# A two-layer decoder trunk on one core: the order of the first loads, early throw-away products, the first shift and scale on TensorE, and the third column chunk on its own

## The chip, the cores and the metric

The kernel runs on one core of one Trainium2 chip. The metric is the device time of one execution in microseconds; the median of three runs is compared.

## The reference, cut to what matters

The input is x, 256 rows of 1,024 numbers, and a conditioning vector c. Two layers follow one another, each an attention and a gated feed-forward part. All of it is float32. Before each attention and each feed-forward part the rows are normed, scaled and shifted; scale and shift come from c:

```python
c_act = jax.nn.silu(c)
for i in range(DEPTH):                                   # DEPTH = 2
    mod = (c_act @ ada_w[i] + ada_b[i])[:, None, :]      # 1024 x 6144 weights for each layer
    sh_a, sc_a, g_a, sh_f, sc_f, g_f = jnp.split(mod, 6, axis=-1)
    h = rms_norm(x, norm_g[i, 0]) * (1.0 + sc_a) + sh_a
    y = moba_attention(h, ...) if i % 2 == 0 else diff_attention(h, ...)
    x = x + g_a * rms_norm(y, norm_g[i, 1])
    h = rms_norm(x, norm_g[i, 2]) * (1.0 + sc_f) + sh_f
    x = x + g_f * rms_norm(swiglu(h, ffn_w_in[i], ffn_w_out[i]), norm_g[i, 3])
```

Both attentions begin with h @ w_qkv, 1,024 x 3,072 weights. No row of the first product can be finished before shift and scale (sh_a, sc_a of layer 0) are known for the rows of w_qkv that it uses.

## The kernel before, in words

The 256 rows are two row tiles (t = 0, 1) of 128. A contraction of 1,024 is eight chunks of 128 (k = 0 to 7). A weight tile is loaded as float32 and split in two parts that add up to it: ACT copies the first part (line 470), VectorE subtracts (line 471). Each product is three matmuls of up to 512 columns (line 479): first part by first part, and the two mixed ones.

`first_block` (lines 664 to 688) makes q (512 columns), k (512 columns) and a third chunk, 512 more columns of q, for both row tiles. It goes over the contraction in blocks of 1, 2, 2, 2 and 1 chunks: (0, 1), (1, 2), (3, 2), (5, 2), (7, 1). For each block `ada_first` makes shift and scale of just these 128 or 256 columns: it loads the two column strips of ada_w for all 1,024 rows of c in pieces of 256 KB (line 413), multiplies the eight row chunks by their part of c and adds them up in one tile a, the first on ACT (line 383), the other seven on VectorE (line 385), and PE sums a over the partitions with a product by a column of ones (line 397). `shift_scale` adds ada_b (tile abc) and the norm's weight (tile ngc) and gives scsh (lines 374 and 377). `modulate` applies scsh to the normed, transposed x (tile xT) and splits the result into the parts of h, tile hq (ACT lines 495 and 500, VectorE line 501). Then come the products of the block, tile pq; each step of them uses the weights of q, k and the third chunk together. The third chunk is loaded for two contraction chunks at once (`qk1`).

x itself is loaded (line 314), squared and summed on ACT (line 529), its root taken on GpSimd (lines 458 to 461), scaled on VectorE (tile xh, line 509), transposed on PE (tile ph, line 326) and copied by ACT to xT (line 671). c, norm_g and ada_b come as small tiles c8, ng and ab (lines 310 to 312), are transposed on PE and copied to cact, ngc and abc (lines 333 to 335).

No order of instructions is written out by hand. `Schedule` holds all operations with an estimated cost each and gives every engine its order by list scheduling, ten passes forward and backward with a fixed seed; the order that comes out best by its estimates is issued. Each engine works its list in order; all loads go through SP's queue, small ones too. Tiles share slots by class (`raw` for loads, `ring` for split weights, `s2`, `bc` and `a` in PSUM, and so on), so that an operation can also wait for a slot. Changing one estimate can change the order everywhere in the program.

After the first block follow the rest of k, then v, the softmax, the output projection, and a feed-forward part of six column chunks; then the same for layer 1. The later shifts, scales and gates (`ada`) are summed on VectorE too, beside the products.

Of the kernel before, what the change touches and what calls it, by code (L numbers as in the profile page):

```python
# [18 lines left out]
D = 1024  # L19
# [27 lines left out]
class Buf:  # L47
    """A tile in a slot of `cls`, taken by its first operation and free after its last; kept when cls is None."""
# [9 lines left out]
class Op:  # L58
    """One or more instructions of an engine, with the estimated cost."""
    __slots__ = ("eng", "cost", "fn", "preds", "succs", "n", "prio", "thin", "start", "end", "bufs", "act", "main", "ready",  # L60
                 "idx", "name")


class Schedule:
    """Operations in program order with what they read and write. `best` gives every engine its order,
    by list scheduling over estimated costs (us)."""

    def __init__(self, slots):
        self.ops, self.slots = [], slots

    def op(self, eng, cost, fn, r=(), w=(), act=None, main=False, name=None, thin=False):
        o = Op()
        o.eng, o.cost, o.fn, o.act, o.main, o.name = eng, cost, fn, act, main, name
        o.thin, o.preds, o.succs, o.bufs, o.idx = thin, set(), [], [], len(self.ops)
        for items, wr in ((r, False), (w, True)):
# [22 lines left out]
    def latest(self):  # L98
        """latest starts before the main products"""
        main = None  # L100
        for o in reversed(self.ops):
            e = min((s.prio - self.latency(o, s) for s in o.succs), default=0.0)
            if o.main:
                e, main = min(e, main.prio if main else e), o
            o.prio = e - (o.cost + 2.5 if o.eng == "SP" else o.cost if o.eng == "PE" else o.cost * STRETCH)

    def turn(self):
        """the same schedule with time reversed"""
# [4 lines left out]
    def run(self, byprio=False):  # L113
# [19 lines left out]
        order, act = [], None  # L133

        def when(o):
            """when o can start, or None while a slot's release isn't known"""
# [15 lines left out]
        while len(order) < len(ops):  # L152
            soon, moved = [], False
            for e in ENGINES:
# [12 lines left out]
                o = min((o for _, o in can), key=lambda o: (o.prio, o.idx))  # L167
                if e in ("ACT", "DVE"):
# [7 lines left out]
                if e == "SP":  # L176
                    at[e] = now + 0.57
# [41 lines left out]
    def best(self):  # L219
        """Rounds of scheduling with time running forward and backward, each with the other's times as priorities."""  # L220
        rng, best = random.Random(SEED), None
        self.latest()
        for i in range(ROUNDS):
            for back in (False, True):
                if back:
                    self.turn()
                for _ in range(4):
                    try:
                        order = self.run(i > 0 and not back)
# [37 lines left out]
def trunk_kernel(ctx: ExitStack, tc: tile.TileContext, x, c, rel_bias, ada_w, ada_b, norm_g, moba_w_qkv, moba_w_o,  # L267
# [52 lines left out]
    def transposes(dst, dkey, blocks, r, main=False):  # L320
        """blocks: list of (column offset in dst, function giving the source)"""
# [5 lines left out]
        op("PE", 0.108 * len(blocks), f, r=list(r) + [ident], w=[(dst, dkey)], main=main, name="tr")  # L327

# [40 lines left out]
    def shift_scale(r, pg, off, l, j, k0, n):  # L369
        """columns of sums -> shift, or the norm's weight times one plus the scale"""  # L370
# [24 lines left out]
    def colsums(pg, off, a, blocks):  # L395
        for i, b in enumerate(blocks, off):
            op("PE", 0.215, lambda i=i, b=b: nc.tensor.matmul(pg[:, i:i + 1], b(), ones1.t[:], start=True, stop=True),  # L397
               r=[a, ones1], w=[(pg, K(i))], thin=True)
# [3 lines left out]
    def ada_first(k0, n):  # L402
        """shift and scale of the first norm for n contraction chunks from k0"""
        m = n * 128
        a = Buf(f"a0{k0}", "s2", [128, 2, m])
        pg = Buf(f"pg0{k0}", "bc")
        q = 4 // n
        for kc in range(0, KC, q):
# [8 lines left out]
        colsums(pg, 0, a, [lambda j=j, b=b: a[:, j, b * 128:b * 128 + 128] for j in range(2) for b in range(n)])  # L417
# [37 lines left out]
    def rstd(m0, n=1, w=1, m1=None):  # L455
        """from m0/n, or from the sum of m0 and m1, the means' halves"""
# [8 lines left out]
    def wpair(name, src, off, seg, kstride, n=512):  # L465
        """rows off.. of 128, two segments of n columns `seg` apart, in two parts that add up to them"""
# [389 lines left out]
```

## Time and profile before

| what | value |
|---|---|
| time of three runs | 650.39, 650.85, 650.94 us, median 650.85 us |
| span of the profiled execution, first to last instruction | 649.0 us, 1.85 us below that median |
| TensorE (PE) busy | 624.0 us, 96% |
| VectorE (DVE) busy | 467.5 us, 72% |
| ScalarE (ACT) busy | 374.4 us, 58% |
| moved by DMA | 160.6 MB, 247 GB/s over the span |

The span is that of one profiled execution; the times are of runs without a profile. Busy is the time in which an engine works at least one instruction. PEld is the loading of the stationary operand and runs beside PE.

### The profile page before, as it was taken

Reading aid. Unit: us, or ns where it says so; the run is one execution under the profiler, and the core shown is the slowest. Engines: PE = TensorE matmul, PEld = TensorE weight load, DVE = VectorE, ACT = ScalarE, POOL = GpSimd, SP = SyncE. Lnnn points to the kernel's source line nnn. Section 1 sums busy time; section 2 is a strip of 40 time slices with the busy share of each in tenths; the row PEclk is TensorE's granted clock in tenths of the full one; section 3 lists DMA queues with packets and bytes.
Section 4 is the critical chain, followed back from the end, with each engine's and each line's share of the span. In section 5 each row is a group of like instructions: output and inputs, shape, how many; then the busy total and the mean of one; then the engine's idle time right before and its main releaser. Section 6 shows DMA issues by size and latency. Waiting matters only on the chain.

```text
span 649.0 us, 8664 instructions
## 1 busy us (share of the span) xinstructions
PE 624.0 (96%) x3069; PEld 517.9 (80%) x3069; DVE 467.5 (72%) x587; ACT 374.4 (58%) x628; POOL 29.9 (5%) x66
## 2 busy tenths in 40 slices
PE   1799999999999999999999999999999999999996
PEld 1687878888788888888988877888888888888894
DVE  3988499997887786757588889896756454587353
ACT  3658779488373535524388878846845253444341
POOL 1000000021000000000020000211100000000001
PEclk9999999999999999999999999999999999999999
DMA  8999999999989697849558847582674738294501
GB/s 276 363 351 314 295 350 352 362 292 284 362 294 369 191 395 254 302 141 317 183 193 293 294 141 268 165 289 66 228 259 114 276 105 283 74 385 144 210 1 65
DMA packets 72488, 160.60 MB, mean 247 GB/s; under 512 B 5491, under 2 KB 22516, under 8 KB 72444
## 3 DMA queue, kind: packets, MB, share of 16 engines
q1 hardware_dynamic: 72444, 160.04, 72.1%
q8 instruction: 24, 0.39, 0.2%
q14 instruction: 20, 0.16, 0.1%
HBM read 158.69 MB, written 1.33 MB: 247 GB/s over the span
## 4 chain that ended last, share of the span: by engine, by line
PE 89%; DMA 5%; ACT 2%; DVE 1%; SPq 1%; issue 1%; DVEq 0%; POOLq 0%; POOL 0%; ACTq 0%
PE pf L479 19%; PE pg L479 17%; PE pu L479 17%; PE pq L479 13%; PE po L479 7%; PE pv L479 6%; PE po L636 2%; PE ps L590 2%; PE pa L326 1%; PE pgc L397 1%; DMA sg<-in_diff_subln_g_dram 1%; DMA x<-in_x_dram 1%; DMA bias<-toep 1%; PE ppt L326 1%; PE pqk L326 1%; DMA aw<-in_ada_w_dram 1%
## 5 line engine op out<-in xcount | busy, mean ns | idle before, releaser
L479 PE MATMUL pg<-s_i,h 128*128 128x512 f32 (+1 forms) x576 | 212.3, 375 | 0.0
L479 PE MATMUL pu<-s_i,h 128*128 128x512 f32 (+1 forms) x576 | 210.8, 373 | 0.0
L479 PE MATMUL pf<-s_u,a 128*128 128x512 f32 x528 | 128.6, 395 | 1.6 <-ACT a L770 1.6
L479 PEld LDWEIGHTS pu<-s_i,h 128*128 128x128 f32 x576 | 108.5, 188 | 19.1
L479 PEld LDWEIGHTS pg<-s_i,h 128*128 128x128 f32 x576 | 108.4, 188 | 19.2
L471 DVE TENSOR_TENSOR s_i<-w_i,s_i 128x1024 fp32r<-128x1024 f32 (+1 forms) x96 | 107.1, 1134 | 20.7 <-ACT s_i L470 17.4
L479 PEld LDWEIGHTS pf<-s_u,a 128*128 128x128 f32 x528 | 98.1, 188 | 23.5 <-ACT a L770 2.0
L470 ACT ACTIVATE s_i<-w_i 128x1024 fp32r<-128x1024 f32 (+1 forms) x96 | 93.0, 985 | 39.4 <-PE pf L479 17.7
L385 DVE SCALAR_TENSOR_TENSOR acc<-aw,cact,acc 128x1024 f32<-128x1024 f32 x70 | 89.2, 1280 | 7.0 <-DMA aw<-in_ada_w_dram 5.8
L471 DVE TENSOR_TENSOR s_u<-w_u,s_u 128x1024 fp32r<-128x1024 f32 x44 | 53.0, 1223 | 29.0 <-ACT s_u L470 28.0
L470 ACT ACTIVATE s_u<-w_u 128x1024 fp32r<-128x1024 f32 x44 | 45.7, 1057 | 36.3 <-PE pu L479 23.1
L770 ACT ACTIVATE a<-pa 128x512 fp32r<-128x512 f32 (+1 forms) x24 | 13.4, 562 | 74.6 <-PE pa L326 74.5
L479 PE MATMUL po<-s_o,o 128*128 128x512 f32 x192 | 48.2, 398 | 0.0
L479 PE MATMUL pq<-s_q,h 128*128 128x512 f32 x192 | 47.5, 398 | 0.0
L771 DVE TENSOR_TENSOR a<-pa,a 128x512 fp32r<-128x512 f32 (+1 forms) x24 | 15.3, 646 | 40.5 <-ACT a L770 40.2
L479 PEld LDWEIGHTS pq<-s_q,h 128*128 128x128 f32 x192 | 35.1, 188 | 7.9 <-issue 0.3
L471 DVE TENSOR_TENSOR s_q<-w_q,s_q 128x1024 fp32r<-128x1024 f32 x32 | 38.5, 1219 | 3.5 <-ACT s_q L470 3.5
L479 PEld LDWEIGHTS po<-s_o,o 128*128 128x128 f32 x192 | 35.2, 188 | 6.8
L470 ACT ACTIVATE s_q<-w_q 128x1024 fp32r<-128x1024 f32 x32 | 33.2, 1058 | 7.7 <-DMA w_q<-in_moba_w_qkv_dram 6.3
L479 PE MATMUL pq<-s_q,hq 128*128 128x512 f32 x144 | 37.3, 417 | 0.0
L479 PEld LDWEIGHTS pq<-s_q,hq 128*128 128x128 f32 x144 | 28.4, 201 | 6.6 <-issue 0.6
L458 POOL TENSOR_SCALAR ms<-ss 128x1 f32<-128x1 f32 x16 | 8.4, 528 | 512.2 <-ACT z L529 501.2
(124 smaller groups left out, 708.3 us busy)
## 6 DMA issues: line engine op xcount, KB each, us to landing
aw<-in_ada_w_dram SPq DMA_DIRECT2D x80, 512.0 KB
w_i<-in_ffn_w_in_dram SPq DMA_DIRECT2D x80, 512.0 KB
w_u<-in_ffn_w_out_dram SPq DMA_DIRECT2D x44, 512.0 KB
aw<-in_ada_w_dram SPq DMA_DIRECT2D x32, 256.0 KB
w_q<-in_moba_w_qkv_dram SPq DMA_DIRECT2D x16, 512.0 KB
w_q<-in_diff_w_qkv_dram SPq DMA_DIRECT2D x16, 512.0 KB
w_q0v<-in_moba_w_qkv_dram SPq DMA_DIRECT2D x8, 512.0 KB
w_o<-in_moba_w_o_dram SPq DMA_DIRECT2D x8, 512.0 KB
```

The lines of the kernel that those rows point to most:

```text
L326: nc.tensor.transpose(dst[:, o:o + n], a, ident[:n, :n])
L385: op("DVE", tt(n) + 0.065, lambda: nc.vector.scalar_tensor_tensor(a.t, w(), cact[:, kc:kc + 1], a.t, op0=OP.mult, op1=OP.add), r=[cact, w. ...
L397: op("PE", 0.215, lambda i=i, b=b: nc.tensor.matmul(pg[:, i:i + 1], b(), ones1.t[:], start=True, stop=True), r=[a, ones1], w=[(pg, K(i))], ...
L458: op("POOL", 0.16, lambda: nc.gpsimd.tensor_scalar(ms.t, m0.t[:], 1.0 / n, EPS, op0=OP.mult, op1=OP.add), r=[m0], w=[ms])
L470: op("ACT", ac(2 * n), lambda: nc.scalar.activation(b[:, 0], w.t[:], AF.Copy), r=[w], w=[(b, K(0))], name="hi" + name)
L471: op("DVE", tt(2 * n), lambda: nc.vector.tensor_sub(b[:, 1], w.t[:], b[:, 0].bitcast(F)), r=[w, (b, K(0))], w=[(b, K(1))], name="lo" + name)
L479: nc.tensor.matmul(p[:, :n], a, b[:, 1 if q == 1 else 0, s], start=first and q == 0, stop=last and q == 2)
L590: nc.tensor.matmul(p[:, i * nk:i * nk + nk], qT[rows, h0 + i, t * 128:t * 128 + 128], kT[rows, h0 + i, 0:nk], start=True, stop=True)
L636: nc.tensor.matmul(p[:, i * 128:i * 128 + 128], a, b, start=kt == 0, stop=kt == t)
L770: op("ACT", ac(n, 0, True), lambda: nc.scalar.activation(a[:, 0, :m], pv(), AF.Copy), r=[p], w=[(a, KR(0, m))])
L771: op("DVE", tt(n), lambda: nc.vector.tensor_sub(a[:, 1, :m], pv(), a[:, 0, :m].bitcast(F)), r=[p, (a, KR(0, m))], w=[(a, KR(10, m))])
```

## The change

The small tile c8 heads SP's queue, followed by the first row tile of x; ab and ng are now issued by ACT's queue. For this an operation has a `boost`, which the forward pass looks at before anything else, and a mark `dma` for loads that another engine than SP issues. Ten products of a tile of ones by itself are added, with the lowest boost, so that PE's list holds them where nothing else can be put. `ada_first` sums the first block (k0 = 0) on PE: 128 columns of ada_w as the stationary operand by one column of c, eight row chunks into one PSUM column each for shift and scale; the additions on ACT and VectorE and the tile a are gone there. The later blocks keep them. In `first_block` the products of the third column chunk are operations of their own, behind those of q and k for both row tiles. Three estimates of the scheduling change: a product, an addition and a column sum cost a little more; and the first activation table counts as loaded. Comments are dropped.

```diff
-    def op(self, eng, cost, fn, r=(), w=(), act=None, main=False, name=None, thin=False):
+    def op(self, eng, cost, fn, r=(), w=(), act=None, main=False, name=None, thin=False, boost=0, dma=False):
...
-        order, act = [], None
+        order, act = [], "silu"
...
-                o = min((o for _, o in can), key=lambda o: (o.prio, o.idx))
-                if e in ("ACT", "DVE"):
+                o = min((o for _, o in can), key=lambda o: (0 if back else -o.boost, o.prio, o.idx))
+                if e in ("ACT", "DVE") and (back or not o.boost):
...
-    op("SP", 0.02, lambda: nc.sync.dma_start(c8.t, dram(c, 0, [[128, KC], [1, 128]])), w=[c8])
-    op("SP", 0.1, lambda: nc.sync.dma_start(ng.t, dram(norm_g, 0, [[128, 64], [1, 128]])), w=[ng])
-    op("SP", 0.15, lambda: nc.sync.dma_start(ab.t, dram(ada_b, 0, [[128, 96], [1, 128]])), w=[ab])
+    op("SP", 0.02, lambda: nc.sync.dma_start(c8.t, dram(c, 0, [[128, KC], [1, 128]])), w=[c8], boost=9)
+    op("ACT", 0.1, lambda: nc.scalar.dma_start(ab.t, dram(ada_b, 0, [[128, 96], [1, 128]])), w=[ab], boost=9, dma=True)
+    op("ACT", 0.1, lambda: nc.scalar.dma_start(ng.t, dram(norm_g, 0, [[128, 64], [1, 128]])), w=[ng], boost=8, dma=True)
     for t in range(T):
-        op("SP", ld(D * 512), lambda t=t: nc.sync.dma_start(xt[t].t, dram(x, t * 128 * D, [[D, 128], [1, D]])), w=[xt[t]])
+        op("SP", ld(D * 512), lambda t=t: nc.sync.dma_start(xt[t].t, dram(x, t * 128 * D, [[D, 128], [1, D]])), w=[xt[t]],
+           boost=(8, 0)[t])
...
+    warm = Buf("warm", "bc")
+    for _ in range(10):
+        op("PE", 0.215, lambda: nc.tensor.matmul(warm.t[:].rearrange("p (a b) -> p a b", a=4), ones.t[:],
+                                                 ones.t[:, None, :].to_broadcast([128, 4, 128]), start=True, stop=True),
+           r=[ones], w=[warm], boost=-99, name="warm")
...
-            op("DVE", tt(n) + 0.065, lambda: nc.vector.scalar_tensor_tensor(a.t, w(), cact[:, kc:kc + 1], a.t, op0=OP.mult,
+            op("DVE", 0.24 + 1.02e-3 * n, lambda: nc.vector.scalar_tensor_tensor(a.t, w(), cact[:, kc:kc + 1], a.t, op0=OP.mult,
...
     def ada_first(k0, n):
         m = n * 128
-        a = Buf(f"a0{k0}", "s2", [128, 2, m])
+        pe = 0 if k0 == 0 else KC
+        a = Buf(f"a0{k0}", "s2", [128, 2, m]) if pe else None
...
+                es = [e for e in range(q) if kc + e >= pe]
+                def f(w=w, j=j, kc=kc, es=es):
+                    for b in range(n):
+                        for e in es:
+                            nc.tensor.matmul(pg[:, n * j + b:n * j + b + 1], w[:, e, j, b * 128:b * 128 + 128], cact[:, kc + e:kc + e + 1],
+                                             start=kc + e + j + b == 0, stop=not pe and kc + e == KC - 1, skip_group_check=True)
+                if es:
+                    op("PE", 0.224 * len(es) * n, f, r=[cact, (w, K(j))], w=[pg], name="ada0")
             for e in range(q):
-                madd(a, View(w, lambda w=w, e=e: w[:, e]), kc + e, 2 * m)
-        colsums(pg, 0, a, [...])
+                if kc + e < pe:
+                    madd(a, View(w, lambda w=w, e=e: w[:, e]), kc + e, 2 * m)
+        if pe:
+            colsums(pg, 0, a, [...])
...
-        cost = len(ps) * (n * 0.4167e-3 + 0.0025)
+        cost = len(ps) * (n * 0.4167e-3 + 0.0133)
...
             for t in range(T):
                 for k in ks:
-                    mm(ps[t], h[t], k, W[k - k0] + [W2[k]], 512, k == 0, k == KC - 1)
+                    mm(ps[t][:2], h[t], k, W[k - k0], 512, k == 0, k == KC - 1)
+            for t in range(T):
+                for k in ks:
+                    mm(ps[t][2:], h[t], k, [W2[k]], 512, k == 0, k == KC - 1)
```

## Rows read from the trace of the kernel before

**Rows 1.** The page: busy time of PE, share of the span and instructions.
```profile
PE 624.0 (96%) x3069; PEld 517.9 (80%) x3069; DVE 467.5 (72%) x587; ACT 374.4 (58%) x628; POOL 29.9 (5%) x66
```

**Rows 2.** Windows: stretch, its length, busy time by engine, granted clock, DMA.
```profile
core 0: us, PE busy (x) PEld busy (x) DVE busy (x) ACT busy (x) POOL busy (x), PEclk, DMA share, GB/s
0.00:23.70 23.70, 7.16 (x30) 5.74 (x30) 13.13 (x26) 11.19 (x23) 3.48 (x16) 1.00 0.95 302
23.70:63.00 39.30, 39.30 (x170) 31.76 (x171) 34.76 (x60) 27.55 (x43) 0.00 (x0) 1.00 1.04 350
63.00:170.00 107.00, 104.73 (x542) 87.36 (x541) 88.10 (x108) 80.89 (x155) 7.85 (x12) 1.00 0.94 319
```

**Rows 3.** Waits of PE over the run: total us, times, longest.
```profile
PE ph L326 <- DVE xh L509: 7.3, 2, 7.1
...
PE pf L479 <- ACT a L770: 1.6, 1, 1.6
```

**Rows 4.** The chain that ended last, 0 to 64 us: start, us, what.
```profile
34.42 0.79 PE pg L397 x8
...
45.00 9.75 PE pq L479 x42
```

**Rows 5.** Timeline of all engines, 0 to 30 us, PE's rows: start, us.
```profile
22.38 1.44 PE L397 MATMUL pg<-ones,a 128*128 128x1 f32 x6 [2.71 <-DVE a L385]
...
23.69 1.63 PE L479 MATMUL pq<-s_q,hq 128*128 128x512 f32 x3
...
25.39 4.92 PE L479 MATMUL pq<-s_q,hq 128*128 128x512 f32 x12
```

**Rows 6.** Timeline, 0 to 30 us, issues on SP's queue.
```profile
0.72 1.55 SPq L413 DMA_DIRECT2D aw<-in_ada_w_dram  x3
...
2.77 0.39 SPq L413 DMA_DIRECT2D aw<-in_ada_w_dram  x1
3.20 0.46 SPq L314 DMA_DIRECT2D x<-in_x_dram  x1
...
9.29 0.59 SPq L311 DMA_DIRECT2D ng<-in_norm_g_dram  x1
...
10.95 0.33 SPq L312 DMA_DIRECT2D ab<-in_ada_b_dram  x1
```

**Rows 7.** Instructions by line and shape, 0 to 25.3 us.
```profile
L385 DVE SCALAR_TENSOR_TENSOR a<-aw,cact,a 128x256 f32<-128x256 f32 x7 | 3.4, 484 | 7.6 <-ACT a L383 7.0 <-DMA aw<-in_ada_w_dram 0.5
```

**Rows 8.** Timeline, 0 to 30 us, rows of DVE and ACT.
```profile
7.03 1.52 DVE L385 SCALAR_TENSOR_TENSOR a<-aw,cact,a 128x256 f32<-128x256 f32 x3 [7.03 <-ACT a L383]
...
9.29 0.63 ACT L529 ACTIVATE xh<-x 128x512 f32<-128x512 f32 x1 [2.30 <-DMA x<-in_x_dram]
...
13.85 0.63 ACT L529 ACTIVATE xh<-x 128x512 f32<-128x512 f32 x1 [2.61 <-DMA x<-in_x_dram]
...
15.09 0.58 ACT L671 ACTIVATE xT<-ph 128x512 f32<-128x512 f32 x1
...
18.43 0.26 DVE L335 COPY abc<-pc 128x96 f32<-128x96 f32 x1
...
19.96 0.49 ACT L500 ACTIVATE hq<-hm 128x128 fp32r<-128x128 f32 x2
...
26.87 0.42 ACT L500 ACTIVATE hq<-hm 128x256 fp32r<-128x256 f32 x1
```

**Rows 9.** DMA issues over the run by line, count, KB each.
```profile
aw<-in_ada_w_dram SPq DMA_DIRECT2D x32, 256.0 KB
w_q<-in_moba_w_qkv_dram SPq DMA_DIRECT2D x16, 512.0 KB
...
x<-in_x_dram SPq DMA_DIRECT2D x2, 512.0 KB
```

**Rows 10.** Windows of the head, columns as in Rows 2.
```profile
0.00:10.00 10.00, 0.24 (x1) 0.18 (x1) 1.45 (x3) 2.67 (x6) 0.96 (x10) 1.00 0.76 228
10.00:20.00 10.00, 5.60 (x22) 4.24 (x22) 7.98 (x19) 5.91 (x15) 2.52 (x6) 1.00 1.09 352
20.00:47.50 27.50, 25.12 (x107) 21.04 (x108) 24.83 (x41) 17.41 (x30) 0.00 (x0) 1.00 1.09 359
```

More of the change, by code (lines that the diff above doesn't have):

```diff
@@ L60 @@
     __slots__ = ("eng", "cost", "fn", "preds", "succs", "n", "prio", "thin", "start", "end", "bufs", "act", "main", "ready",
-                 "idx", "name")
+                 "idx", "name", "boost", "dma")
 class Schedule:
@@ L69, in __init__ @@
         self.ops, self.slots = [], slots
-    def op(self, eng, cost, fn, r=(), w=(), act=None, main=False, name=None, thin=False):
+        self.boost = 0
+    def op(self, eng, cost, fn, r=(), w=(), act=None, main=False, name=None, thin=False, boost=0, dma=False):
         o = Op()
@@ L74, in op @@
         o.thin, o.preds, o.succs, o.bufs, o.idx = thin, set(), [], [], len(self.ops)
+        o.boost, o.dma = self.boost + boost, dma
         for items, wr in ((r, False), (w, True)):
@@ L104, in latest @@
                 e, main = min(e, main.prio if main else e), o
-            o.prio = e - (o.cost + 2.5 if o.eng == "SP" else o.cost if o.eng == "PE" else o.cost * STRETCH)
+            o.prio = e - (o.cost + 2.5 if o.eng == "SP" or o.dma else o.cost if o.eng == "PE" else o.cost * STRETCH)
     def turn(self):
@@ L111, in turn, with run @@
             o.preds, o.succs, o.idx = o.succs, o.preds, i
-    def run(self, byprio=False):
+    def run(self, byprio=False, back=False):
         ops = self.ops
@@ L176, in run @@
                 if e == "SP":
+                    at[e] = now + 0.57
+                    dma = max(dma, at[e]) + o.cost
+                    o.end = dma + 1.9
+                elif o.dma:
                     at[e] = now + 0.57
@@ L228, in best @@
                     try:
-                        order = self.run(i > 0 and not back)
+                        order = self.run(i > 0 and not back, back)
                         break
@@ L308, in trunk_kernel @@
     ab = Buf("ab", "PT0", [96, 128])
-    op("SP", 0.02, lambda: nc.sync.dma_start(c8.t, dram(c, 0, [[128, KC], [1, 128]])), w=[c8])
-    op("SP", 0.1, lambda: nc.sync.dma_start(ng.t, dram(norm_g, 0, [[128, 64], [1, 128]])), w=[ng])
-    op("SP", 0.15, lambda: nc.sync.dma_start(ab.t, dram(ada_b, 0, [[128, 96], [1, 128]])), w=[ab])
+    S_.boost = 0
+    op("SP", 0.02, lambda: nc.sync.dma_start(c8.t, dram(c, 0, [[128, KC], [1, 128]])), w=[c8], boost=9)
+    op("ACT", 0.1, lambda: nc.scalar.dma_start(ab.t, dram(ada_b, 0, [[128, 96], [1, 128]])), w=[ab], boost=9, dma=True)
+    op("ACT", 0.1, lambda: nc.scalar.dma_start(ng.t, dram(norm_g, 0, [[128, 64], [1, 128]])), w=[ng], boost=8, dma=True)
     for t in range(T):
-        op("SP", ld(D * 512), lambda t=t: nc.sync.dma_start(xt[t].t, dram(x, t * 128 * D, [[D, 128], [1, D]])), w=[xt[t]])
+        op("SP", ld(D * 512), lambda t=t: nc.sync.dma_start(xt[t].t, dram(x, t * 128 * D, [[D, 128], [1, D]])), w=[xt[t]],
+           boost=(8, 0)[t])
     op("POOL", 0.5, lambda: make_identity(nc, ident.t), w=[ident])
@@ L335, in trunk_kernel @@
     op("DVE", 0.17, lambda: nc.vector.tensor_copy(abc.t, pc[:, 256:352]), r=[(pc, K(2))], w=[abc])
+    S_.boost = 0
     toep = Buf("toep", t=dr.tile([H, NCOPY, NTOEP], F, name="toep"))
@@ L396, in colsums @@
         for i, b in enumerate(blocks, off):
-            op("PE", 0.215, lambda i=i, b=b: nc.tensor.matmul(pg[:, i:i + 1], b(), ones1.t[:], start=True, stop=True),
+            op("PE", 0.224, lambda i=i, b=b: nc.tensor.matmul(pg[:, i:i + 1], b(), ones1.t[:], start=True, stop=True),
                r=[a, ones1], w=[(pg, K(i))], thin=True)
@@ L414, in ada_first @@
                     w[:, :, j], dram(ada_w, kc * 128 * 6 * D + j * D + k0 * 128, [[6 * D, 128], [128 * 6 * D, q], [1, m]])), w=[(w, K(j))])
+                es = [e for e in range(q) if kc + e >= pe]
[6 more added lines that the diff above has]
+                    op("PE", 0.224 * len(es) * n, f, r=[cact, (w, K(j))], w=[pg], name="ada0")
             for e in range(q):
-                madd(a, View(w, lambda w=w, e=e: w[:, e]), kc + e, 2 * m)
-        colsums(pg, 0, a, [lambda j=j, b=b: a[:, j, b * 128:b * 128 + 128] for j in range(2) for b in range(n)])
+                if kc + e < pe:
+                    madd(a, View(w, lambda w=w, e=e: w[:, e]), kc + e, 2 * m)
+        if pe:
+            colsums(pg, 0, a, [lambda j=j, b=b: a[:, j, b * 128:b * 128 + 128] for j in range(2) for b in range(n)])
         for j in range(2):
@@ L675, in first_block @@
         W2 = []
-        for k0, n in ((0, 1), (1, 2), (3, 2), (5, 2), (7, 1)):
+        for i, (k0, n) in enumerate(((0, 1), (1, 2), (3, 2), (5, 2), (7, 1))):
             ada_first(k0, n)
@@ L686, in first_block @@
                 for k in ks:
-                    mm(ps[t], h[t], k, W[k - k0] + [W2[k]], 512, k == 0, k == KC - 1)
+                    mm(ps[t][:2], h[t], k, W[k - k0], 512, k == 0, k == KC - 1)
+            for t in range(T):
+                for k in ks:
+                    mm(ps[t][2:], h[t], k, [W2[k]], 512, k == 0, k == KC - 1)
+        S_.boost = 0
         return h, ps
```

## The prediction

> **What bounds the kernel now.** I read first the engine totals and the table by stretch. PE is busy 624.0 of 649.0 us [rows 1]; the stretches say where it is not: 7.16 us of work in the first 23.7 us, then 39.30 of 39.30 us, 2.27 us idle between 63 and 170 us [rows 2]. What is left of the 624.0 us, 472.9 us, is all of the time from 170 to 642.9 us, and the 6.1 us after that are a tail without PE. The list of PE's waits agrees: 7.3 us for the normed x at the start, and later 1.6 us, once, for a part of the gated activations [rows 3]. So PE's stream of products sets the end, and only three things can move it: when the stream begins, what it loses while it runs, the tail. The tail and the number of 512-column products are not touched.
>
> Does the stream run at its full pace? 42 products take 9.75 us, 0.232 us each [rows 4]. The 18 products of the first contraction chunk do not: they begin at 23.69 us, twelve of them take 4.92 us, 0.41 us each, the fifteenth ends at 30.31 [rows 5], so the 18th at about 30.8. The granted clock is shown as 1.00 there too [rows 2], but 0.41 us for 512 columns is the pace of the lower level, 1.2 GHz (0.427 us), not of 2.4 GHz (0.213 us). Whatever came before in scattered pieces had not raised it.
>
> Then the head, engine by engine. x's first tile is issued at 3.20 us behind four weight loads and lands at 9.29 [rows 6]. The weight chunks for the first shift and scale are added up on VectorE in seven steps of 0.484 us [rows 7], mixed with those of the second block. And abc, the transposed ada_b that scsh needs, is there only at 18.43 + 0.26 us, because ab is issued at 10.95 us [rows 6, 8]. Then PE stands 2.71 us, to 22.38 us, before the second block's column sums, which wait for VectorE's last addition [rows 5], though the first block's hq is ready at 20.45 us [rows 8].
>
> **The change, part by part.** *Small loads and x first.* c leaves at about 0.7 us, x's first tile at about 1.2 us. Before, x took 6.1 us from issue to landing with four loads of 256 KB (1.05 MB) ahead of it [rows 6, 9]. The first 20 us show 228 and 352 GB/s [rows 10]; at some 300 GB/s 1.05 MB are 3.5 us, so x takes 2.6 us without them: 4 to 5.5 us, I take 5. From landing to the first half of the transposed x took 6.4 us (9.29 to 15.09 + 0.58) [rows 8]; at that rate it is there at about 11.4 us. ab and ng move to ACT's queue: SP is spared 0.59 + 0.33 us of issuing [rows 6], ACT gets the like at its start, when it has nothing to do until c is through PE (ACT works 2.67 us of the first 10, [rows 10]). Without that cover it would be 1 us. The Trainium skill says in "DMA: Bandwidth & Descriptors", Issuing engines are not separate DMA queues, that transfers of all issuing engines share the same sixteen engines, so that only issue time is saved; no run here has shown ACT issuing yet. My sum counts no bandwidth for it either.
>
> *Throw-away products.* Ten of 512 columns, at 0.43 us at most 4.3 us, as soon as the ones are written; PE has 16.5 us to spare before 23.7 us [rows 2]. Cost 0 to 0.4 us (one such product ahead of c's transposition), I take 0. Their gain is what the clock does afterwards: 0, if it is low again when the real products come, up to 2.2 us (12 x 0.18) if it stays. I take 0: they are over by about 6 us, and the rows show that scattered work up to 23.7 us did not keep the clock up. The Trainium skill, "TensorE: Matmul & The Clock Gate", What's actually happening, speaks against this part: the low level is the default, sustained work lifts it, and an idle stretch brings it back. By that rule the ten products bring nothing to the main stream; the slow twelve [rows 5] agree.
>
> *First 128 rows on PE.* VectorE loses seven steps of 0.484 us, 3.4 us [rows 7], and ACT one of about the same. PE gets 16 products of one column instead of two. A one-column product is two matmul instructions here, at 0.10 us (eight in 0.79 us, [rows 4]) to 0.24 us (six in 1.44 us, low clock, [rows 5]): 32 instructions, 3.2 to 7.7 us, all in idle time but the last load's four products, 0.8 to 1.9 us, which replace 4 x 0.48 us on VectorE and its two sums. The four loads stand behind c and x: 1.57 MB, at 2.28 MB in 10 us about 8 us, taken 9; with 1.9 us of products and the 1.8 us that lay between abc and hq before (18.69 to 20.45, [rows 8]) the first product is possible at about 13 us: 12 to 16, before 23.69.
>
> *Third column chunk separate.* The 144 products remain 144. The first twelve of the block no longer wait for the second weight load. Its cost is nothing but the order.
>
> *What then is late.* Row tile 1 of x, which was there at 13.85 us and gave its hq by 20.45 us [rows 8]. It is not moved ahead, so its nine products start at about 20 and end at about 24 us at the low pace. The second block comes out at the same: its additions ended just before 22.38 us, with VectorE nearly full (7.98 and 9.96 us of 10 from 10 and 20 us on, [rows 10]); four of the seven 0.484 us steps (all but the three from 7.03 us on, [rows 8]) stood between them and go, 1.9 us, so 20.4; sums 1.44 [rows 5], 1.8 from there to hq as above and two hops make 3.6 us: 24.0 us. Bounds: 22 us, if loads alone decide (c, two x tiles, four and eight loads of 256 KB and two of 512 KB are 5.2 MB, in at 18.3 us by [rows 10], and 3.6 us behind); 27.3 us, where the second block's first hq was before [rows 8].
>
> **The sum.** What remains after the first 18 products is a full stream in both. It began at 30.8 us and now at 24.0: 6.8 us. Off for the clock, if it falls between the first block and the second: 0 to 2.6 us, I take 1.0, nearer to zero because the second tile's products lead up to it. Off for supply: the first stage needs 15.7 MB (32 x 256 KB, 12 of the 16 x 512 KB, two x tiles, [rows 9]), which at the rates of [rows 10] are in at some 47.5 us, before their use at some 51 us; but PE already waits for 2.3 us between 63 and 170 us at a DMA share of 0.94 [rows 2], which may double: 0 to 2.3, I take 0.8. Gain 5.0 us: span 644.0 us, and with the 1.85 us between this span and the median of 650.85 us, 645.9 us. The larger planned costs of products and additions only reorder; on a full PE I count 0, and give the danger to a rival.
>
> **Rivals.** *The second block waits as long as before* (27.3 us; loads late, PE idle and slow again): 30.8 - 27.3 - 2.6 = 0.9 us, 649.9 us, between 648.8 and 650.8. For it: DMA runs at 352 to 362 GB/s from 10 us on [rows 10]. Against: VectorE, not DMA, was what the additions waited for.
> *The clock stays and loads decide:* 22.0 us, nothing off, 8.8 us: 642.0 us. The Trainium skill's rule on the clock, cited above, is against it; the rows on twelve slow products too.
> *Handed back later:* the gain comes, but between 63 and 170 us PE waits for weights until the old time: 650.85 us. Against: VectorE works 88.1 of 107 us there and DMA 0.94 [rows 2], so there is room.
> *Slower: a new order in the feed-forward part.* The wait of 1.6 us named above [rows 3]. The changed costs replan every engine; should this wait come at further chunk changes, from four of them on (6.4 us) the gain of 5.0 us is gone and the time 652.3 us, with six 655.5. Against: it came once in the whole run.
>
> **How the numbers follow.** Chances: forecast 0.62, late second block 0.13, clock and loads at their best 0.12, handed back 0.06, slower 0.07. The forecast itself spans 643 to 648.8 us. The range from 641.8 to 650.0 us takes in the best case's time and most of the late block's, and leaves out about 2 in 10. About 0.2%, 1.3 us, is what a measurement can tell from no change: faster below 649.55 us. The late block falls about half on either side of this. Faster 0.62 + 0.12 + 0.06 = 0.80, same 0.07 + 0.06 = 0.13, slower 0.07.
>
> **What would show it.** After: x landing at about 5 us; scsh at about 11; first product of 512 columns at 12 to 16 us; the 19th at about 24, and the last of the stage's 144 some 5 to 6 us before the 62.9 us of now; PE's idle time from 63 to 170 us (before the shift) still 2 to 3 us; last product at about 638 us. If the slow pace shows in the products after 24 us, the clock term was too small; if PE has holes in the first stage, loads bind; if the first stage gains and the end does not, it was handed back and PE's waits name where.

## The result and the profile after

The changed kernel takes 658.0 us (median of four runs, 657.38 to 659.78), beside 650.89 us for the kernel before on the same chip: ratio 1.0104 [1.0085, 1.0123], 1.0% slower. Forecast were 645.9 us, and a range from 641.8 to 650.0. The profiled execution took 657.6 us, its span is 655.8, 6.8 longer than before's 649.0.

PE's waits first (engine, line, releaser: total us, times, longest), which answer to [rows 3]:

```profile
PE ppt L334 <- ACT sx L639: 2.7, 2, 2.5
PE pg L415 <- DVE a L403: 1.9, 1, 1.9
PE warm L341 <- POOL ones L324: 1.6, 1, 1.6
PE po L511 <- DVE o L684: 1.2, 1, 1.2
PE pc L334 <- DMA ab<-in_ada_b_dram: 1.0, 1, 1.0
PE ph L334 <- DVE z L541: 0.8, 2, 0.5
...
PE pot L334 <- DVE on L676: 0.6, 1, 0.6
...
PE pf L511 <- ACT a L806: 0.5, 1, 0.5
```

The 7.3 us at the start are gone, and so is most of the 1.6 us in the feed-forward part. New are two waits of layer 1's attention, 1.2 us for `o` and 0.6 us for `on`, and 2.7 us for a softmax in layer 0. (Of PE's tiles, ps holds the score products, ppt the transposed softmax, pot the transposed normed output of layer 1's attention, pk and pv the products for the rest of k and for v, po those of the output projection, pg and pu the first and pf the last products of the feed-forward part; pg is also the tile of the column sums in the head.) The windows, columns as in [rows 2]:

```profile
0.00:23.70 23.70, 18.55 (x71) 15.87 (x72) 10.34 (x20) 10.80 (x23) 2.85 (x16) 1.00 0.97 313
23.70:63.00 39.30, 39.30 (x178) 31.87 (x177) 35.51 (x60) 29.80 (x47) 0.00 (x0) 1.00 1.05 359
63.00:170.00 107.00, 103.45 (x532) 86.69 (x531) 88.11 (x108) 77.72 (x151) 7.37 (x12) 0.98 0.93 315
...
139.00:142.00 3.00, 3.00 (x10) 2.42 (x9) 2.90 (x6) 2.97 (x7) 0.56 (x1) 0.51 0.99 276
```

PE is busy 637.9 us (97%), 13.9 more, and yet the kernel is slower. 11.4 of them lie in the first 23.7 us (18.55 less 7.16). So a fuller PE says nothing here; where the time went is told by when the same work is reached. First or last start of groups of products, us:

| | before | after | later by |
|---|---|---|---|
| first product of the first stage | 23.7 | 23.0 | -0.7 |
| last product of it (pq) | 62.6 | 60.2 | -2.4 |
| rest of k done (pk) | 77.6 | 74.8 | -2.8 |
| v done (pv, layer 0) | 109.1 | 107.9 | -1.2 |
| feed-forward part begins (pg, layer 0) | 141.5 | 142.9 | +1.4 |
| layer 1 begins (pq) | 337.4 | 337.1 | -0.3 |
| its last pq | 392.6 | 393.2 | +0.6 |
| its last po | 453.7 | 460.0 | +6.3 |
| last product of all (pf) | 642.5 | 649.2 | +6.7 |

The head's gain is 2.4 to 2.8 us here and is all but gone when layer 1 begins. Most of the loss, 5.7 us, arises between 393 and 460 us, in layer 1's attention; 0.9 us arise just before it, in q and k of layer 1.

**The head.** PE's timeline of the changed kernel:

```profile
1.62 2.50 PE L341 MATMUL warm<-ones 128*128 128x512 f32 x5 [1.62 <-POOL ones L324]
...
5.67 2.48 PE L341 MATMUL warm<-ones 128*128 128x512 f32 x5
...
10.84 3.58 PE L441 MATMUL pg<-cact,aw 128*128 128x1 f32 x16
...
16.01 3.41 PE L441 MATMUL pg<-cact,aw 128*128 128x1 f32 x16
21.28 1.83 PE L415 MATMUL pg<-ones,a 128*128 128x1 f32 x8 [1.85 <-DVE a L403]
22.97 10.92 PE L511 MATMUL pq<-s_q,hq 128*128 128x512 f32 x41
```

and DVE's and ACT's:

```profile
5.28 0.63 ACT L561 ACTIVATE xh<-x 128x512 f32<-128x512 f32 x1 [0.45 <-DMA x<-in_x_dram]
...
6.90 0.72 ACT L401 ACTIVATE a<-aw,cact 128x512 f32<-128x512 f32 x1 [0.29 <-DMA aw<-in_ada_w_dram]
...
20.26 0.15 DVE L395 SCALAR_TENSOR_TENSOR scsh<-scsh,ngc 128x1 f32<-128x1 f32 x1
...
21.86 0.29 ACT L532 ACTIVATE hq<-hm 128x128 fp32r<-128x128 f32 x1
```

x landed by 5.28 us (forecast 5). But at 6.90 us ACT works on strips of 128x512: these are the *second* block's. The new plan loads them ahead of the first block's, whose products by columns of c run only at 10.84 and 16.01 us. The 32 instructions take 3.58 + 3.41 = 7.0 us, 0.22 each, within the forecast 3.2 to 7.7. scsh is there at 20.4 us instead of 11, the first part of hq at 22.15, and in PE's list the second block's eight column sums stand before the first product and wait 1.85 us for VectorE.

**Layer 1's attention.** PE's instructions by shape from the last pq to the last po (x count | busy us, mean ns | idle before), of the kernel before, 392.6 to 454.2 us:

```profile
L479 PE MATMUL pv<-s_q1v,h 128*128 128x512 f32 x96 | 24.1, 399 | 0.0
L479 PE MATMUL po<-s_o,o 128*128 128x512 f32 x96 | 23.0, 394 | 0.0
...
L326 PE MATMUL pot<-ident,on 128*128 128x128 f32 x16 | 2.4, 274 | 0.0
L590 PE MATMUL ps<-kT,qT 64*128 64x256 f32 x16 | 2.3, 402 | 0.0
```

and of the changed one, 393.2 to 460.5 us:

```profile
L511 PE MATMUL pv<-s_q1v,h 128*128 128x512 f32 x96 | 24.5, 399 | 0.0
L511 PE MATMUL po<-s_o,o 128*128 128x512 f32 x96 | 23.3, 394 | 1.2 <-DVE o L684 1.2
...
L622 PE MATMUL ps<-kT,qT 64*128 64x256 f32 x16 | 4.5, 402 | 0.0
...
L334 PE MATMUL pot<-ident,on 128*128 128x128 f32 x16 | 3.0, 288 | 0.6 <-DVE on L676 0.6
...
L334 PE MATMUL pqk<-ident,qk 128*128 128x128 f32 x8 | 1.1, 285 | 0.2 <-ACT qk L602 0.2
```

The same instructions in the same number. The score products ps take 2.2 us more at the same mean of 402 ns, PE waits 2.0 us, pot takes 0.6, pv 0.4 and po 0.3 more; four smaller groups take 0.5 less. That is 5.0 of the 5.7 us. Why sixteen equal instructions take twice the time is seen in PE's timeline, first of before:

```profile
399.36 1.14 PE L590 MATMUL ps<-kT,qT 64*128 64x256 f32 x8
```

then of the changed kernel:

```profile
399.87 1.13 PE L622 MATMUL ps<-kT,qT 64*128 64x256 f32 x4
...
402.44 1.13 PE L622 MATMUL ps<-kT,qT 64*128 64x256 f32 x4
```

A score product has two halves of 64 rows each, on different rows of the array. Side by side, both take 1.14 us together; with other instructions between them, 1.13 us each. The Trainium skill, "TensorE: Matmul & The Clock Gate", Part 3 (The mechanism), says that products on different row groups overlap in the array; this trace agrees. Of layer 1's six score products the new order has four apart (three of 64x256), the old order one (of 64x128): 3 x (2.26 - 1.14) = 3.4 us in the whole layer.

### The profile page after: what moved, and what is told of

Its sections match the earlier page's. It is cut to its first block, busy times and chain, and to the rows that moved or that the text cites. A ratio compares the mean times of both kernels' runs of the same rounds, so it can differ in the third digit from the quotient of the medians.

```text
span 655.8 us, 8739 instructions
## 1 busy us (share of the span) xinstructions
PE 637.9 (97%) x3107; PEld 528.5 (81%) x3107; DVE 465.2 (71%) x580; ACT 373.5 (57%) x627; POOL 35.8 (5%) x66
## 4 chain that ended last, share of the span: by engine, by line
PE 62%; issue 14%; DMA 10%; ACT 5%; DVE 5%; POOL 2%; SPq 0%; DVEq 0%; POOLq 0%; ACTq 0%
PE pg L511 16%; PE pu L511 16%; PE pf L511 16%; PE pq L511 5%; DMA aw<-in_ada_w_dram 4%; PE po L511 3%; DVE acc L403 2%; DMA bias<-toep 2%; ACT s_i L502 1%; POOL y L493 1%; PE pa L334 1%; ACT z L561 1%; DMA w_i<-in_ffn_w_in_dram 1%; DMA w_q0v<-in_moba_w_qkv_dram 1%; PE ph L334 1%
## 5 line engine op out<-in xcount | busy, mean ns | idle before, releaser
L490 POOL TENSOR_SCALAR ms<-ss 128x1 f32<-128x1 f32 x16 | 10.3, 646 | 517.7 <-ACT z L561 510.1
L511 PE MATMUL pq<-s_q,hq 128*128 128x512 f32 x144 | 35.5, 405 | 0.0
```

The source lines that it names most:

```text
L490: op("POOL", 0.16, lambda: nc.gpsimd.tensor_scalar(ms.t, m0.t[:], 1.0 / n, EPS, op0=OP.mult, op1=OP.add), r=[m0], w=[ms])
L511: nc.tensor.matmul(p[:, :n], a, b[:, 1 if q == 1 else 0, s], start=first and q == 0, stop=last and q == 2)
```

## The experiments

Each time was taken beside runs of the kernel before on the same chip, and the ratio of the two is what is compared. "Old order" means: the kernel's planner is run on the kernel before, all lists and slots are kept, and only the changed operations are put into them at places named in the diff.

| run | order | parts of the change | us | ratio |
|---|---|---|---|---|
| est_only | new | none | 666.35 | 1.0226 [1.0202, 1.0250] |
| before_other_seed | new | none | 659.31 | 1.0126 [1.0084, 1.0168] |
| after_other_seed | new | all | 660.12 | 1.0126 [1.0104, 1.0149] |
| parts_old_est | new | all, old estimates | 655.24 | 1.0071 [1.0047, 1.0096] |
| pairs_together | new, halves joined | all | 655.56 | 1.0064 [1.0041, 1.0087] |
| layer1_old_order | new, layer 1 old | all | 666.22 | 1.0225 [1.0190, 1.0259] |
| head_new_rest_old | old behind the head | all | 649.3 | 0.9959 [0.9938, 0.9980] |
| parts_kept_order | old | all | 649.46 | 0.9971 [0.9956, 0.9986] |
| kept_no_throwaway | old | without throw-away products | 650.7 | 0.9976 [0.9956, 0.9996] |
| kept_loads_only | old | loads | 650.08 | 0.9973 [0.9952, 0.9994] |
| kept_loads_separate | old | loads, third chunk | 648.9 | 0.9938 [0.9913, 0.9963] |
| loads_third_chunk_pairs_scsh | old, two moves | loads, third chunk | 650.61 | 0.9992 [0.9975, 1.0009] |
| before_halves_apart | old, halves apart | none | 656.76 | 1.0084 [1.0060, 1.0108] |

**A new order without the change.** est_only is the kernel before with only the new estimates, before_other_seed with another seed of the planner's noise, after_other_seed the same for the changed kernel.

```diff
-        order, act = [], None
+        order, act = [], "silu"
-            op("DVE", tt(n) + 0.065, lambda: nc.vector.scalar_tensor_tensor(a.t, w(), cact[:, kc:kc + 1], a.t, op0=OP.mult,
+            op("DVE", 0.24 + 1.02e-3 * n, lambda: nc.vector.scalar_tensor_tensor(a.t, w(), cact[:, kc:kc + 1], a.t, op0=OP.mult,
...
-            op("PE", 0.215, lambda i=i, b=b: nc.tensor.matmul(pg[:, i:i + 1], b(), ones1.t[:], start=True, stop=True),
+            op("PE", 0.224, lambda i=i, b=b: nc.tensor.matmul(pg[:, i:i + 1], b(), ones1.t[:], start=True, stop=True),
...
-        cost = len(ps) * (n * 0.4167e-3 + 0.0025)
+        cost = len(ps) * (n * 0.4167e-3 + 0.0133)
```
```diff
-ROUNDS, NOISE, SEED = 5, 0.2, 142
+ROUNDS, NOISE, SEED = 5, 0.2, 143
```

> The kernel before with only the changed estimates of the schedule (products, additions, column sums, first table counted as loaded); no load, product or addition is changed. Theory 1, the order made anew is what costs (in the changed kernel layer 1's attention takes 6 us longer with the same operations): this order is as new, so the time moves by several us from 650.9 although no work changed, 653 to 658 us. Theory 2, the changed parts themselves cost: within 1.3 us of 650.9.

> The kernel before, word for word, but the planner's random seed is 143 instead of 142: the same operations in another order with an estimate as good. Theory 1, a new order by itself costs, since the order of before is a good draw: 653 to 666 us, half of layer 1's six score pairs torn apart (four of six here), 1 us each. Rival, the order matters only with the changed estimates: 650 to 652 us.

> The changed kernel with SEED 143 in place of 142: the same operations and estimates, another order of equal planned length. Score halves apart in layer 1: three of six, by 4, 2 and one position. Theory, that the loss is an accident of the order: a time that differs from 658.0 us by more than 0.3 per cent, in either direction, between 650 and 664 us. Rival, that the four parts themselves cost 1 per cent: 657 to 659 us.

Nothing was computed otherwise in the first two, and they are 2.3 and 1.3% slower: more than the whole loss of the change. before_other_seed lies in the range of its theory, est_only (666.35 us) above the 658 us that its theory allowed: the direction was forecast, the size was not. The two longest of PE's waits in est_only behind the head:

```profile
PE ph L352 <- DVE z L567: 4.9, 2, 4.3
PE ps L648 <- ACT kT L630: 3.0, 1, 3.0
```

after_other_seed, 660.1 us, is 0.3% from 658.0, at the edge of what the theory asked for, and above the rival's 657 to 659. By the ratios the two differ by 0.2%, with intervals that overlap, so this run decides nothing; it lies as high (1.0126) as the same seed does without the change.

One rival stands beside all of these runs. In the middle of an execution the granted clock falls to 0.50 for a few microseconds, and how often differs between executions of one and the same kernel: the mean granted clock of the kernel before lies between 0.987 and 0.999. This does not make the difference: among executions with the same mean granted clock of 0.994 the kernel before takes 651.3 to 652.7 us (beside est_only), the changed one 657.4 and 658.4, est_only 664.1.

**The change without the new order.** parts_kept_order has all four parts in the old order; head_new_rest_old has the changed kernel's own order up to the end of the first stage and the old one behind it; parts_old_est is the changed kernel with the old estimates, so with a third order.

```diff
+    put(0, "c8", "ab", "ng", "x0")            # the loads, ahead of the weights
+    put(keys.index("c8 transposed"), *warm)   # ten throw-away products
-    first block's additions and column sums
+    put(their places, "ada0 by columns of c")
+    put(behind the products of q and k, "those of the third chunk")
+    move("second block's column sums", "first block's products")
```

> All four parts set by hand into the order and the slots of the kernel before; outside the first stage every engine keeps the list of before. Theory 1: the head's gain comes and is kept, less what the softmax behind the bias takes back: 646 to 649.5 us, and layer 1 as long as before. Theory 2: 651 us or more. The forecast of 645.9 us would be met if block two began at 24 us and nothing were handed back.

> The changed kernel with its own planned order up to the end of the first stage (loads, throw-away products, the first 128 rows on PE, the third chunk apart), and everything behind it in the order of the kernel before. Theory, that the order behind the head costs and the four parts do not: between 648.5 and 650.5 us, ratio 0.996 to 1.000, last product pq at about 60.2 us as in the changed kernel, layer 1 as before. Rival, that the head itself costs later on (by loads that are late or slots that come free late): 653 us or more, with PE's waits between 63 and 170 us well above the 2.3 us of before.

> The changed kernel with the estimates of before: all four parts, another order. Theory 1 (the order costs): some time between 648 and 660 us that differs from 658.0 by 2 us or more, with layer 1's attention not 6 us longer or longer for other operations. Theory 2 (the parts cost): 657 to 659 us, with the loss in the same places.

With the old order, or the old order behind the head alone, the same four parts are 0.3 to 0.4% *faster* than before. Both runs lie in the ranges of their first theories, though head_new_rest_old with its last pq at 61.1 us and not 60.2, and layer 1's attention takes 61.1 and 61.0 us, as before. The slots were dealt anew in head_new_rest_old, so it isn't the old slots that make it fast. The changed kernel's own head costs nothing in layer 1's attention, as a window of head_new_rest_old shows:

```profile
395.00:455.00 60.00, 60.00 (x333) 50.58 (x332) 49.82 (x85) 41.15 (x82) 10.12 (x17) 1.00 0.57 186
```

parts_old_est, the third order, is 2.8 us from 658.0, as its first theory asked. Its attention of layer 1 takes 65.8 us, 4.7 more than before, without a wait of PE there; five of its six score products have their halves apart.

**The parts one by one, in the old order.** kept_no_throwaway leaves out the ten products, kept_loads_separate the sums on PE too (VectorE sums as before), kept_loads_only the separate chunk as well and, with it, the last move above: its second block's column sums stand ahead of the first products.

> Loads first, first block's sums on PE and third chunk separate in the order of before, without the throw-away products. With them (649.5 us) c's transposition began at 5.67 us, behind all ten, and the clock had fallen again by 9 us. Theory 1, they bring the stream nothing and hold c: first product 1 to 2 us earlier than 19.49 us and 648 to 649.5 us. Rival, the clock they raise is worth something: 650 us or more.

> Only the small loads and x's first tile ahead (ab and ng from ACT, transposed and copied behind c), the rest in the order of before. abc is early, but PE's list still has the second block's column sums ahead of the products, and these wait for VectorE: first product 21 to 23 us (before 23.69), 649.5 to 651 us. Rival, the loads are the whole gain of the kept order: 649.5 us or less with a first product at 20 us.

> Loads first and third chunk separate, its first products ahead of the second block's sums, order of before; the first block's sums stay on VectorE and nothing is thrown away. If sums on PE are worth their 7 us of one-column products, this is slower than the run without throw-away products by 1 us or more and has its first product later than 19.5 us. Rival, VectorE does them as early: the same time within 0.7 us.

The throw-away products bring nothing that shows: 0.9971 with and 0.9976 without. In microseconds kept_no_throwaway (650.7) lies in its rival's range, and its first product came 0.5 us earlier (19.0 us) and not 1 to 2; the overlapping ratios bear out neither side. kept_loads_only came as expected, 650.1 us with a first product at 21.9. The sums on PE bring no gain that shows: 0.9976 with and 0.9938 without. Neither side of that expectation came, as the run without them is 1.8 us faster. All lie between 0.9938 and 0.9976; their intervals overlap, and no ranking among them is claimed. None brings the forecast 5 us. A windows row and PE's timeline of kept_loads_separate show one reason:

```profile
23.70:63.00 39.30, 37.44 (x173) 29.76 (x173) 35.75 (x60) 29.81 (x47) 0.00 (x0) 1.00 1.04 348
```
```profile
19.73 3.92 PE L629 MATMUL pq<-s_q,hq 128*128 128x512 f32 x8 [0.59 <-ACT hq L650]
...
28.05 2.14 PE L629 MATMUL pq<-s_q,hq 128*128 128x512 f32 x8 [0.73 <-DVE s_q L621]
```

Its first product starts 4.0 us earlier than before, eight of them take 0.49 us each, and PE then stands 1.86 us in a stretch that was full. Its last pq starts at 61.0 us. The other reason is the clock. In parts_kept_order the first product starts at 19.5 us, and the granted clock stays at 0.50 until 28.9 us:

```profile
8.50:28.90 20.40, 19.60 (x74) 17.57 (x75) 15.70 (x30) 13.24 (x29) 1.88 (x6) 0.50 1.08 361
```

In the runs with the parts the first product starts between 18.4 and 23.7 us and the last pq between 60.2 and 63.0, and an earlier first is no earlier last.

**Layer 1.** pairs_together is the changed kernel in its own order with the halves of each score product side by side; before_halves_apart puts them apart in the kernel before; layer1_old_order is the changed kernel with layer 1 in the old order.

```diff
     for a, b in the two halves of each score product of layer 1:
+        move(b, a)                       # pairs_together: a, and what needs it, up to b
+        move(b, the next other product)  # before_halves_apart: one product between a and b
```

> The changed kernel in its own order, but in layer 1 the score products of a head group's two halves (64 rows each) follow one another on PE again, where its order had set products between them (four of six pairs). In the rows four products of 64x256 take 1.06 us by themselves and eight of both halves 1.08 us. If that is most of what layer 1 lost: three pairs of 64x256 at 1.06 and one of 64x128 at 0.55 us give 3.7 us, 654.3 us. Rival: the halves only shift a wait that the softmax has anyway, 657 to 658 us.

> The kernel before in its own order and slots, but in layer 1's attention one product of another kind is put between the two 64-row halves of the five score products whose halves follow each other (three of 64x256, two of 64x128). Theory, that halves that follow each other run together and pay once: 3 x 1.04 + 2 x 0.55 = 4.2 us more, about 655 us, ratio 1.006. Rival, that the halves only take turns in what the records show and their place is free: no change, 0.999 to 1.001.

> The changed kernel in its own order through layer 0, and layer 1 in the order of the kernel before. Theory, that the 6 us of layer 1's attention come from its order (halves of the score products apart, 3.7 us, and waits of 2.3 us): about 652 us, ratio 1.002, and pv of layer 1 ends about 84 us after the last pq of layer 0's feed-forward part hands over, as before. Rival, that layer 1 is longer because something of layer 0 arrives late: 656 to 658 us, ratio 1.008 or more.

before_halves_apart changes nothing but five places in PE's list. Its timeline:

```profile
401.93 1.13 PE L738 MATMUL ps<-kT,qT 64*128 64x256 f32 x4
402.99 0.73 PE L627 MATMUL pv<-s_q1v,h 128*128 128x512 f32 x2
403.65 1.13 PE L738 MATMUL ps<-kT,qT 64*128 64x256 f32 x4
```

The five are four of 64x256 and one of 64x128, not three and two as the expectation counted: 4 x 1.12 + (2 x 1.16 - 1.71) = 5.1 us. The time grew by 0.84%, 5.5 us [3.9, 7.0], and layer 1, from its first pq to its last po, by 5.5 us (116.3 to 121.8). The distance of the halves has a price by itself. The span grew by 5.1 us too, but that is in part chance: in this execution the clock was low from 138.0 to 141.4 us, in layer 0, and in before's it wasn't.

Joined in the changed kernel, they gave back 0.40% (1.0104 to 1.0064), 2.6 us, between the expectation's 3.7 us and its rival. Layer 1, the only part that this edit touches, says more: from its first pq to its last po it takes 122.9 us in the changed kernel and 119.2 with the halves joined, 3.7 us less, as expected, and no stretch of low clock lies in either. The span shrank by only 2.0 us (655.8 to 653.8) because layer 0, whose lists are the same in both, took 2.3 us longer in that execution. What is left of layer 1's loss, 119.2 against 116.3 us, is 2.9 us; the waits for `o` and `on`, 1.8 us, are still there.

layer1_old_order missed both expectations by far, 666.2 us. With two plans joined the slots were dealt anew, and at the seam PE stood 5.6 us for kT:

```profile
PE ps L772 <- ACT kT L754: 5.6, 1, 5.6
PE pf L661 <- DVE a L963: 3.0, 1, 3.0
```

The mean granted clock of the profiled execution (670.46 us) is low as well, 0.982 for the changed kernel's 0.996. But from its last pq (413.3 us) to its last po (474.3) it needs 61.0 us, as before (453.7 - 392.6 = 61.1) and not 66.8 as the changed kernel. For the stretch in dispute it bears out the order; for the total it says only what one more order can cost.

**A better version.** loads_third_chunk_pairs_scsh adds to kept_loads_separate that the first block's scsh stands right behind its sums and that the one pair apart is joined.

```diff
+    move(behind "first block's column sums", "its scsh")
+    move(b, a)   # the one score product of layer 1 that stands apart
```

> The order of the kernel before, with only the loads moved and the third chunk apart (sums on VectorE, no throw-away products), the first block's shift and scale right behind its sums, and the halves of all six score products of layer 1 adjacent. Beside the run of the first two parts alone (648.9 us, ratio 0.9938): the pair that stood apart gives back 0.55 us, the earlier shift and scale 0.5 to 2 us of the first products; 646.5 to 648.5 us, ratio 0.990 to 0.993. Rival, that the stage is bound by loads and the pair by something else: no change, 0.994.

Neither came; the rival was nearer. The first product came at 19.3 us for 19.7, and the joined pair brought PE a new wait for kT:

```profile
PE ps L760 <- ACT kT L742: 1.2, 1, 1.2
```

That outweighs the 0.6 us of the pair. Why this run lies 0.5% above kept_loads_separate is not explained by its trace, whose span is 1.5 us *shorter* (647.3 and 648.8): the profiled execution took 649.15 us here (its twelve runs 649.10 to 653.94) and 650.60 there (its ten 646.98 to 650.81), where the granted clock was low from 136.1 to 142.9 us. The medians, 650.61 and 648.9 us, are 0.3% apart, on two chips. kept_loads_separate is the fastest by its ratio, head_new_rest_old the next; both beat both kernels, by intervals that lie below 1.

## Why the prediction was wrong

**The step that failed** is "The larger planned costs of products and additions only reorder; on a full PE I count 0". An order is not free on a full PE. Here it cost about 9 us: the same four parts are at 1.0104 in the new order and at 0.9959 with the old order behind the head, 0.0145 x 651 = 9.4 us, and a new order without any part costs 1.3 or 2.3%. That is most of the 12.1 us between forecast and measurement; another 2.3 are the head, which brought 2.7 us (0.0041 x 651) of its 5.0. The price of the order is paid in two ways which the run before hides because its order is a good one: work that runs together only when it is adjacent (3.4 us by the rows, 3.7 in the run that joined all six), and short waits of a full PE for the chain of attention (2.0 us between 393 and 460 us). The rest of the 9.4 us lies in layer 0, in the slower pot, pv and po of layer 1's attention and in its feed-forward part, and was not taken apart.

**The slower rival** had the right agent, a replanned order, and the wrong place. Its wait for the gated activations shrank from 1.6 to 0.5 us; the loss is in layer 1's attention. Its chance of 0.07 was too small: of five orders that the planner made anew in these runs (the changed kernel's, est_only, both other seeds, parts_old_est), every one was slower than the one of before.

**The head's terms.** x at 5 us was right, and so were the throw-away products (cost 0, gain 0, though they ended at 8.2 us and not 6) and the price of the 32 one-column instructions (7.0 us). scsh at 11 and the first product at 13 were wrong by 9 and 10 us: the working kept the first block's strips in front of the queue, and the new plan put the second block's there. The stream's start was the term of 6.8 us. Forty-one products take 10.92 us, the first seven of them 3.2, so that the 19th begins at 22.97 + 3.20 + 11 x 0.227 = 28.7 us, 2.1 earlier than 30.8 instead of 6.8; the stage ends 2.4 earlier and not 5 to 6.

Even of the 2.4 us only 0.7 are the earlier start. The products keep the slow pace until the trace's first record of the clock begins, at 29.5 us in the kernel before and at 25.9 us in the changed one: 5.9 and 2.9 us at half speed, which is another 1.5 us. This part is luck of the execution. pairs_together has the same head in the same order, and its clock rose at 28.7 us, so that the same 41 products take 12.30 us there for 10.92 and its last pq starts at 61.5 us:

```profile
22.88 12.30 PE L633 MATMUL pq<-s_q,hq 128*128 128x512 f32 x41
```

And with a start earlier still (19.0 to 19.7 us in the old order, 18.4 in parts_old_est) the stage did not end earlier: the low clock lasted until 27.8 to 28.9 us, or PE found holes (1.9 us in kept_loads_separate). The prediction had the full pace from 24.0 us on; in parts_kept_order it came at 28.9, and 4.9 us at half speed cost 2.5 us for the 1.0 that it took. The holes of kept_loads_separate stand behind VectorE's s_q and a, for which the sum has no term in the stream.

**Handed back.** The prediction gave this 0.06, and for layer 0 it is in part what happened, through a softmax and not through waits for weights. The first softmax of layer 0 starts no earlier, as the timeline of DVE and PE shows, in the changed kernel

```profile
75.25 0.69 DVE L625 TENSOR_TENSOR sx<-ps,bias 128x512 f32<-128x512 f32 x1 [2.63 <-PE pk L511]
...
81.27 0.44 PE L334 MATMUL ppt<-ident,sx 128*128 128x128 f32 x2 [2.54 <-ACT sx L639]
...
133.32 1.62 PE L415 MATMUL pgc<-ones,acc 128*128 128x1 f32 x14
...
136.04 1.84 PE L415 MATMUL pgc<-ones,acc 128*128 128x1 f32 x16
...
139.11 3.63 PE L511 MATMUL po<-s_o,o 128*128 128x512 f32 x9
```

and before

```profile
75.09 0.69 DVE L593 TENSOR_TENSOR sx<-ps,bias 128x512 f32<-128x512 f32 x1 [4.67 <-DMA bias<-toep]
```

so that PE, 2.8 us ahead, waits 2.54 us. And at 133 to 138 us the new order has thirty one-column sums in two bunches; from 139 to 142 us the granted clock is 0.51 (windows above), the lower level of 1.2 GHz, and nine products take 3.63 us, 0.40 each. That looks like a price of the bunches, but the clock also falls there in the old order: before_halves_apart has the lists of the kernel before in layer 0, and in its execution and in before's the same stretch reads

```profile
138.00:141.40 3.40, 3.40 (x12) 2.85 (x12) 2.66 (x7) 2.03 (x6) 0.00 (x0) 0.50 0.80 279
```
```profile
138.00:141.40 3.40, 3.40 (x20) 2.88 (x21) 2.90 (x10) 2.35 (x7) 0.07 (x1) 1.00 0.83 283
```

So this stretch of low clock is not shown to come from the new order. PE's idle time from 63 to 170 us is 3.55 us, 2.27 before, forecast 2 to 3.

## What to carry to other kernels

Where a planner makes the order, every edit is two edits: the part itself, and a new order for all the rest. Time the new order without the part (another seed, the estimates alone) and the part in the old order before either is judged; here the first was worth +1.3 to +2.3%, the second -0.1 to -0.6%. A planner that gives each product a price of its own (here 0.855 us for each half, wherever it stands) doesn't see what two of them are worth side by side; halves that share the array should be one operation for it. And the effect of an edit is read from the stretch that it touches: the spans of two executions also differ by where the clock rose and fell.

## What the runs showed of the hardware

Two products of 64x256 on 64 rows each cost one when adjacent: 1.14 us against 2 x 1.13, and each instruction's mean, 402 ns, shows nothing of it; only the busy time of the group does. For 64x128 the gain is smaller, 1.71 us against 2 x 1.16. The Trainium skill's "TensorEngine Tiling (Array Packing)", Tiling Modes, says besides that a change of mode drains the engine; no run here separates that.

The granted clock reads 1.00 in the windows of the head although products run at 0.41 to 0.50 us there, and the trace's first record of it begins only at 25.9 us in the changed kernel; before that, only the pace tells the clock. In the changed kernel the ten products left no sign of a raised clock: its one-column instructions take 0.22 us each from 10.84 us on. In parts_old_est, where the ten are split in two fives as well, the record begins earlier; its windows:

```profile
12.00:13.00 1.00, 1.00 (x11) 1.00 (x11) 0.88 (x2) 0.00 (x0) 0.00 (x0) 1.00 1.11 339
...
14.50:27.60 13.10, 11.10 (x35) 9.31 (x35) 9.83 (x21) 8.19 (x16) 0.00 (x0) 0.50 1.08 362
```

and of its timeline

```profile
10.74 2.74 PE L463 MATMUL pg<-cact,aw 128*128 128x1 f32 x24
```

One-column instructions take 0.11 us each there, at 2.4 GHz, instead of 0.22; then the clock falls to 0.50, the 1.2 GHz level, at about 14 us, while PE has worked one-column products and transposes without a hole from 10.7 us on, and stays there until 27.6 us. In parts_kept_order, with all ten in one row from 1.6 to 5.7 us, the clock is low again from 8.5 us (window above), and kept_no_throwaway has no such early record. So the ten products can lift the clock, in some orders and executions, and each time it was lost again before the first product of the stage.
